# Expert activations made ahead of the transposition, one transposition for two experts, and another order of the down products

## The chip, the cores and the metric

The kernel runs on one core of one Trainium2 chip, in float32. The metric is device microseconds of one execution, the median of several runs. The core's engines work side by side and each takes its own instructions in order: TensorE (PE; its weight loads are shown as PEld), VectorE (DVE), ScalarE (ACT) and the queue of SyncE (SP), which issues the loads.

## The reference

One encoder layer on 512 tokens of width 1024: a mixing sub-layer (a gated short convolution and a latent attention), an attention into a memory of 256 rows, a layer of 16 experts, and a last RMSNorm. The change touches the experts alone. Each expert takes the 64 tokens with the largest affinity to it:

```python
def expert_choice_moe(h, w_router, w_gate, w_up, w_down):
    ...
    gates, idx = lax.top_k(jnp.swapaxes(aff, 1, 2), cap)
    xg = jax.vmap(lambda hb, ib: hb[ib])(h, idx)
    a = jax.nn.silu(jnp.einsum("becd,edf->becf", xg, w_gate)) * jnp.einsum("becd,edf->becf", xg, w_up)
    yo = jnp.einsum("becf,efd->becd", a, w_down) * gates[..., None].astype(h.dtype)
    return jax.vmap(lambda ib, vb: jnp.zeros((s, d), vb.dtype).at[ib.reshape(-1)].add(vb.reshape(-1, d)))(idx, yo)
```

## The kernel before

The sub-layers ahead of the experts and the choice of the tokens take the first 680 us. Then the experts run in eight pairs p, experts 2p and 2p + 1. The weights of a pair come as 24 chunks of 1 MiB ([128, 2048] float32), 16 for gate and up and 8 for down, in the order of their use, through SP's queue. Each chunk has one of 22 equal slots; as soon as a slot is given back after its last product, the next chunk is issued into it (`load_experts`). The order of the instructions on each engine is the order in which the code is written (a manual schedule); waits between engines are semaphores. PSUM banks and the scratch tiles (`scr`, eight buffers) are handed out in turn.

What a pair does, in order:

- `gu_half(e, n)`, for expert e and half n of the 1024 hidden columns: TensorE multiplies the gathered tokens XG (64 of them, as weights) with the gate and the up matrix. The gate product goes to partitions 0 to 63 of one bank and the up product to partitions 64 to 127, side by side in the two halves of the array (L1281, L1282): 8 d tiles, two passes each for float32, in two parts of four d tiles (`gu_part`) between which `mid` stands. Then `gu_evac` copies the bank to SBUF on ScalarE (L1289). The first pair has `gu_wide` in its place, which runs both halves side by side (L1310, L1311).
- `act_half(e, n)`: four transposes of 128x128 on TensorE (L1324, tile guT) bring half n of one expert to [f, (gate, up) of 64 places]; then Silu of the gates on ScalarE (L1329) and the product with the up values on VectorE (L1330) give aT[e], the weights of the down products. They run one step late, as `mid` of the next `gu_half`, and the last of a pair inside the down products.
- `gather(p + 1)`: VectorE makes a one-hot matrix oh (L1241) and the same times the rstd, ohr (L1244); TensorE multiplies the rows of x2 with ohr, one d tile a step (L1249), and VectorE puts each step's bank into XG (L1250). Two steps come behind the last `gu_half` of a pair and two behind each of the first three down steps.
- `down(p)`: four steps of 16 matmuls (L1353), two experts side by side in the array, one half n of d after the other and within it the two halves kh of f; ScalarE and VectorE take each finished half of d out of its bank, times the gates, as a high and a low part (L1359, L1360). `mid`, the last `act_half`, stands ahead of the second step, (n, kh) = (0, 1), which needs it at once.
- In the next pair, behind its first `gu_half`: `pair_prep` (L1259, L1266), then `combine` (L1374), which adds the pair's rows to the tokens' accumulators on VectorE (L1376). The last pair has `tail` in place of gather and combine, which adds and normalises the first half of d under the products of the second.

What a pair of `gu_half` products looks like, and what sets the place of `act_half`:

```python
            PE.matmul(b.t[0:64], lt, wg[:, k], start=kk == 0, stop=kk == KT - 1)
            PE.matmul(b.t[64:128], lt, wu[:, k], start=kk == 0, stop=kk == KT - 1)
...
                gu_half(e, 0, mid=(lambda: act_half(e - 1, 1)) if q else None)
...
                gu_half(e, 1, mid=lambda: act_half(e, 0))
```

Of the kernel before, what the change touches and what calls it, by code (L numbers as in the profile page):

```python
# [18 lines left out]
KT = 8          # 128-row tiles of D  # L19
NT = 4          # 128-row tiles of T  # L20
# [5 lines left out]
SLOT = 2048     # float32 elements per partition and slot  # L26
NSLOT = 22
SPLIT_AHEAD = 2
# slots kept back from the experts' weights; order of the steps that are woven into each other
# [6 lines left out]
# columns of the packed small operands  # L36
# [7 lines left out]
# dense weight entries ([128, 1024] each) in the order of their use  # L44
# [19 lines left out]
def layer_kernel(ctx: ExitStack, tc: tile.TileContext, x, mem, small, rope, dense, experts, out):  # L64
# [42 lines left out]
    def mini(dt, name):  # L107
        """4 KB per partition; three at a time"""
        return minip.tile([128, 1024], dt, name=nm(name), tag="mini")
# [7 lines left out]
    def split(src, hi, lo):  # L117
        """src = hi + lo, both of 12 significant bits"""
        A.copy(hi, src)  # L119
        V.tensor_tensor(lo, src, f32(hi), op=OP.subtract)  # L120

    def split_scaled(src, by, hi, lo):
        """src * by = hi + lo"""
        A.activation(hi, src, AF.Copy, scale=by)
        V.scalar_tensor_tensor(lo, src, by, f32(hi), op0=OP.mult, op1=OP.subtract)

# [12 lines left out]
    def prep_steps(upto, ahead, pieces):  # L139
        """split the entries below upto, a piece at a time; have their chunks, and some more, under way"""  # L140
# [38 lines left out]
    def load_spare():  # L179
        """the last chunk of the first expert goes where there is room beside the slots"""  # L180
        xraw[SPARE] = [scr(name="xs") for _ in range(4)]
        for j, t in enumerate(xraw[SPARE]):
            nc.sync.dma_start(t, experts[SPARE][:, j * 512:(j + 1) * 512])

    class Entry:
        """the split weights of one entry; to be freed after its last use"""
# [11 lines left out]
    class Mac:  # L198
        """products that add up in one piece of a bank"""
# [13 lines left out]
    class Proj:  # L213
        """bank[f, t] = sum over d of W[d, f] * act[d, t], for one 128-column tile of W"""
# [60 lines left out]
    def keep_warm(b, n):  # L275
        """products that nobody reads, against the clock gate of the tensor engine"""
        for _ in range(n):
            PE.matmul(b.t, ones, one.to_broadcast([128, 512]), start=True, stop=True)
# [8 lines left out]
    def rstd_parts(ss, width, n=1):  # L287
        """r, t with r * t = 1 / sqrt(ss / width + eps): the table's root and a Newton step"""
# [25 lines left out]
    def transpose_scaled(rows, g, dst):  # L314
        """rows: list of [128, D] tiles; dst[j] = (hi, lo) of [128, len(rows) * 128]; g per d"""
# [13 lines left out]
    def act_slots(n, name):  # L329
        """[128, 2 (hi, lo), 512] pieces, two to a slot"""  # L330
# [173 lines left out]
    def evac_late(f, b, *args):  # L504
        """evacuate a bank one step later, when its products are done"""
# [10 lines left out]
    def values(n, kt):  # L516
        """values of four heads and 128 keys: [keys, 4 * DV]"""
# [43 lines left out]
    def pair_rope(hp):  # L561
        """rotary queries of two heads; [hi; lo] and [lo; hi] over the partitions"""
# [315 lines left out]
    # values of the memory: [keys, D]  # L878
# [166 lines left out]
    def logits(a, half):  # L1045
        """four products side by side: expert e and k % 4 = g on partition 32 * g + e (the others hold no expert)"""
# [15 lines left out]
    def norm2(a):  # L1062
        """rstd of the rows a: a guess from the bits, a Newton step and one of the third order"""
# [39 lines left out]
    # the C largest affinities of each expert so far, in order, and the next ones behind them: partition e has the  # L1103
    # first 64 of each 128 tokens, partition 32 + e the others
# [24 lines left out]
    def weave(g, other, every=1):  # L1129
        """the steps of g; after some of them one of the other"""  # L1130
# [70 lines left out]
    # the two lists have the C largest at the places i and C - 1 - i, whichever is larger  # L1201
# [35 lines left out]
    def gather(p):  # L1237
        """XG[d, (expert, place)] = x2 * rstd * g of the chosen tokens, one d tile at a time"""
# [15 lines left out]
    def pair_prep(p):  # L1254
        """gates and the transposed one-hot of two experts"""
# [16 lines left out]
    gu_sb, aT = {}, {}  # L1272
# [14 lines left out]
    def gu_evac(e, b, n):  # L1287
        s = scr(name="gu")
        A.copy(s, b.t)  # L1289
        b.free()  # L1290
        gu_sb[e, n] = s
# [9 lines left out]
    def gu_wide(e, then):  # L1301
        """the first two experts: all columns of one d tile after the other, so that a chunk is soon free"""
# [16 lines left out]
    def act_half(e, n):  # L1319
        """silu(gate) * up, transposed to [f, place]"""  # L1320
        s = gu_sb.pop((e, n))
        b = Bank("guT")
        for j in range(4):
            PE.transpose(b.t[:, j * 128:(j + 1) * 128], s[:, j * 128:(j + 1) * 128], ident)  # L1324
        w = b.t.rearrange("p (j s c) -> p j s c", j=4, s=2)
        if n == 0:
            aT[e] = scr(name="aT").rearrange("p (k c) -> p k c", k=KT)
        sg = scr(name="sg")[:, 0:256].rearrange("p (j c) -> p j c", j=4)
        A.activation(sg, w[:, :, 0], AF.Silu)  # L1329
        V.tensor_tensor(aT[e][:, n * 4:n * 4 + 4], w[:, :, 1], sg, op=OP.mult)  # L1330
        b.free()

    def down(p, mid, each, then=None):
        """Y[(expert, place), d] of two experts, times the gates; one half of d after the other"""
        ys = Slot(FR, "y")
        yv = ys.v("n s d", n=2, s=2)
        for n in range(2):
            b = Bank(f"y{n}")
            for kh in range(2):
                cs_ = [xraw.popleft(), xraw.popleft()]  # L1340
                if (n, kh) == (0, 1):
                    mid()
                for kk in range(4):
                    if then is not None:
                        then(n, kh * 4 + kk, yv)
                    k = kh * 4 + kk
                    for q in range(2):
                        if (q, n, kk) == (1, 0, 0) and then is not None:
                            bw = Bank("warm")
                            keep_warm(bw, WARM3)  # L1350
                            bw.free()
                        w = cs_[q].v("k d", k=4)
                        PE.matmul(b.t[q * 64:q * 64 + 64], aT[2 * p + q][:, k], w[:, kk],  # L1353
                                  start=k == 0, stop=k == KT - 1)
                for c in cs_:
                    c.free()
                load_experts(RES_X)
                some(each, GB)
            A.activation(yv[:, n, 0], b.t, AF.Identity, scale=gcol[p])  # L1359
            V.scalar_tensor_tensor(yv[:, n, 1], b.t, gcol[p], f32(yv[:, n, 0]), op0=OP.mult, op1=OP.subtract)  # L1360
            b.free()
# [66 lines left out]
    for p in range(NP):  # L1428
        last = p == NP - 1
        for q in range(2):  # L1430
# [4 lines left out]
            if e == 1:  # L1435
                steps = {1: lambda: act_half(0, 0), 3: lambda: act_half(0, 1), 5: lambda: pair_prep(0)}
                gu_wide(1, lambda k: steps.get(k, int)())
            else:
                gu_half(e, 0, mid=(lambda: act_half(e - 1, 1)) if q else None)
# [12 lines left out]
            if e > 1:  # L1452
                gu_half(e, 1, mid=lambda: act_half(e, 0))
# [5 lines left out]
        if p == 0:  # L1459
            act_half(1, 0)  # L1460

        def mid():
            act_half(2 * p + 1, 1)
# [13 lines left out]
    def last_root(a):  # L1477
        """the parts of the rstd of tile a: the root, and the mean"""
# [33 lines left out]
def _colmajor(w):  # L1512
    """[K, 128 * c] -> per 128-column tile: [c, 128 (row in tile), K / 128 * 128]"""
# [4 lines left out]
def _rowpairs(w):  # L1518
    """[1024, 1024] -> entries (column half, row pair): [8, 128, 2 * 512]"""
# [36 lines left out]
def _experts(i):  # L1556
    gu = np.stack([i["w_exp_gate"][0], i["w_exp_up"][0]], 1)              # e, s, d, f
    gu = gu.reshape(E, 2, 2, 4, 128, 2, 512).transpose(0, 5, 2, 1, 4, 3, 6)  # e, n, kh, s, p, k, f
    dn = i["w_exp_down"][0].reshape(E // 2, 2, 2, 4, 128, 2, 512).transpose(0, 5, 2, 1, 4, 3, 6)  # pair, n, kh, q, p, k, d
    out = np.empty((E // 2, PAIR_CHUNKS, 128, SLOT), np.float32)  # L1560
    out[:, :16] = gu.reshape(E // 2, 16, 128, SLOT)
    wide = np.stack([i["w_exp_gate"][0, :2], i["w_exp_up"][0, :2]], 2)     # e, d, s, f
# [58 lines left out]
```

## Time and profile before

| | |
|---|---|
| runs of the kernel before | 1175.21, 1175.72, 1175.77 us; median 1175.72 |
| span of the profiled execution | 1174.3 us |
| busy share of the span | PE 98%, PEld 66%, DVE 41%, ACT 31% |
| mean granted clock of TensorE | 0.992 of full speed |
| chain that ended last, by line | gate and up products 17% (L1281), down products 11% (L1353), gather 5% (L1249) |
| loads of the experts' weights | 189 of 1 MiB and 8 smaller ones; median 12.6 us from issue to landing for the large ones |

The span runs from the first to the last instruction of one profiled execution; the runs are timed without the profiler, and their median is 1.4 us above that span. All stretches are counted in us from the span's start. A busy TensorE is one with a product in its pipeline. The chain of waits is followed back from the last instruction, at each step to what released it, so its rows on one engine follow each other without a gap where nothing else was waited for. Of the first page's slices, the last 17 (from 675 us) are the experts: there DVE and ACT are busy some one or two tenths, DMA and PE nine in nearly all of them.

### The profile page before, as it was taken

The page shows a single profiled execution, that of the slowest core. Times are in us where ns is not written, and L with a number is a line of the kernel's source. Part 1 is how long each engine was busy: PE and PEld are TensorE (multiplying, and loading weights), DVE is VectorE, ACT ScalarE, POOL GpSimd, SP SyncE. Part 2 cuts the span into 40 slices and gives each one's busy share as a digit, 9 for nine tenths or more (in the row PEclk, how much of TensorE's full clock was granted, in tenths as well). Part 3 has the DMA queues.
Part 4 walks back from the last instruction along what each step waited for, and adds up shares of the span by engine and source line. Part 5 has one row for each costly group of instructions (what it writes and reads, how often), then busy time and mean ns, then how long its engine had stood idle before and what let it go on. Part 6 is the DMA issues. An engine that isn't in the chain of part 4 may idle for free.

```text
span 1174.3 us, 14110 instructions
## 1 busy us (share of the span) xinstructions
PE 1150.4 (98%) x5779; PEld 771.9 (66%) x5779; DVE 484.9 (41%) x942; ACT 364.4 (31%) x672; POOL 1.2 (0%) x5
## 2 busy tenths in 40 slices
PE   8999999999999999999999899999999999999995
PEld 6888888888788888898888544444444444444432
DVE  6567443223588755564555721212121212121204
ACT  6223222223798833564334301100000000000013
POOL 0000000000000000000000000000000000000000
PEclk9999999999999999999999899999999999999998
DMA  8233222222000344234244788899999999999941
GB/s 347 72 108 108 72 75 105 108 108 72 1 36 2 119 168 179 72 133 155 72 180 172 311 317 347 328 417 407 421 421 420 421 421 421 421 421 420 422 188 71
DMA packets 38927, 265.95 MB, mean 226 GB/s; under 512 B 4432, under 2 KB 4816, under 8 KB 8016
## 3 DMA queue, kind: packets, MB, share of 16 engines
q1 hardware_dynamic: 38720, 265.00, 57.0%
q8 instruction: 45, 0.74, 0.3%
q14 instruction: 18, 0.15, 0.0%
q10 hardware_dynamic: 144, 0.07, 0.0%
HBM read 262.95 MB, written 2.10 MB: 226 GB/s over the span
## 4 chain that ended last, share of the span: by engine, by line
PE 93%; DVE 3%; ACT 3%; DMA 0%; issue 0%; SPq 0%; DVEq 0%; ACTq 0%
PE gu L1281 17%; PE y L1353 11%; PE xg L1249 5%; PE mm L205 4%; PE mo L205 4%; PE mq L205 4%; PE mix L205 4%; PE co L205 4%; PE gcv L205 4%; PE gb L205 4%; PE gc L205 4%; PE xc L205 4%; PE gml L205 4%; PE gu L1310 2%; PE cb L1374 2%; PE mk L205 2%
## 5 line engine op out<-in xcount | busy, mean ns | idle before, releaser
L1281 PE MATMUL gu<-xw,xg 128*64 128x512 f32 x448 | 199.8, 596 | 0.0
L1282 PE MATMUL gu<-xw,xg 128*64 128x512 f32 x448 | 199.8, 596 | 0.0
L120 DVE TENSOR_TENSOR ent<-raw,ent 128x1024 fp32r<-128x1024 f32 (+2 forms) x113 | 129.1, 1155 | 92.0 <-ACT ent L119 91.9
L1281 PEld LDWEIGHTS gu<-xw,xg 128*64 128x64 f32 x448 | 58.9, 137 | 117.7 <-issue 115.4
L1353 PE MATMUL y<-xw,aT 128*64 128x512 f32 x512 | 127.4, 599 | 0.0
L119 ACT CAST ent<-raw 128x1024 fp32r<-128x1024 f32 (+2 forms) x113 | 109.1, 996 | 0.0
L1353 PEld LDWEIGHTS y<-xw,aT 128*64 128x64 f32 x512 | 35.8, 136 | 69.1 <-issue 59.8
L1250 DVE TENSOR_SCALAR xg<-xg,small 128x128 f32<-128x128 f32 x64 | 22.5, 351 | 141.1 <-PE xg L1249 141.1
L1249 PEld LDWEIGHTS xg<-ohr,x 128*128 128x128 f32 x512 | 59.8, 191 | 28.8 <-issue 21.1
L1330 DVE TENSOR_TENSOR aT<-guT,sg 128x256 f32<-128x256 f32 x32 | 13.6, 425 | 150.3 <-ACT sg L1329 150.3
L1249 PE MATMUL xg<-ohr,x 128*128 128x128 f32 x512 | 66.4, 282 | 0.4 <-DVE ohr L1244 0.4
L1329 ACT ACTIVATE sg<-guT 128x256 f32<-128x256 f32 x32 | 12.3, 384 | 166.1 <-PE guT L1324 166.1
L1289 ACT COPY gu<-gu 128x512 f32<-128x512 f32 x32 | 18.8, 586 | 145.0 <-PE gu L1282 110.9
L1282 PEld LDWEIGHTS gu<-xw,xg 128*64 128x64 f32 x448 | 58.9, 137 | 0.0
L205 PE MATMUL mm<-ent,mo 128*128 128x512 f32 x192 | 48.4, 399 | 0.0
L205 PE MATMUL gcv<-hT,ent 128*128 128x512 f32 x192 | 44.8, 389 | 0.0
L205 PE MATMUL co<-yT,ent 128*128 128x512 f32 x192 | 44.8, 389 | 0.0
L205 PE MATMUL gb<-hT,ent 128*128 128x512 f32 x192 | 44.8, 389 | 0.0
L205 PE MATMUL gc<-hT,ent 128*128 128x512 f32 x192 | 44.8, 389 | 0.0
L205 PE MATMUL xc<-hT,ent 128*128 128x512 f32 x192 | 44.8, 389 | 0.0
L205 PE MATMUL mq<-hm,ent 128*128 128x512 f32 x192 | 44.7, 390 | 0.0
L205 PE MATMUL mo<-o,ent 128*128 128x512 f32 x192 | 44.7, 391 | 0.0
(276 smaller groups left out, 1717.4 us busy)
## 6 DMA issues: line engine op xcount, KB each, us to landing
xw<-in_experts_dram SPq DMA_DIRECT2D x189, 1024.0 KB, 12.6
raw<-in_dense_dram SPq DMA_DIRECT2D x52, 1024.0 KB, 4.8
x<-in_x_dram SPq DMA_DIRECT2D x8, 512.0 KB, 4.5
xw<-in_experts_dram SPq DMA_DIRECT2D x4, 512.0 KB, 16.1
out_dram<-out SPq DMA_DIRECT2D x4, 512.0 KB, 2.6
raw<-in_dense_dram SPq DMA_DIRECT2D x2, 512.0 KB, 8.1
mem<-in_mem_dram SPq DMA_DIRECT2D x1, 1024.0 KB, 5.0
xs<-in_experts_dram SPq DMA_DIRECT2D x4, 256.0 KB, 15.0
```

The costliest lines, as they stand in the source:

```text
L119: A.copy(hi, src)
L120: V.tensor_tensor(lo, src, f32(hi), op=OP.subtract)
L205: PE.matmul(self.o, lhsT, rhs, start=self.k == 0, stop=self.k == self.n - 1)
L1249: PE.matmul(b.t[:, 0:128], xt[a][:, k * 128:(k + 1) * 128], w[:, a], start=a == 0, stop=a == NT - 1)
L1250: V.tensor_scalar(XG[p][:, k], b.t[:, 0:128], col(S_GMOE + k), None, op0=OP.mult)
L1281: PE.matmul(b.t[0:64], lt, wg[:, k], start=kk == 0, stop=kk == KT - 1)
L1282: PE.matmul(b.t[64:128], lt, wu[:, k], start=kk == 0, stop=kk == KT - 1)
L1289: A.copy(s, b.t)
L1310: PE.matmul(bs[n].t[0:64], lt, w[n], start=k == 0, stop=k == KT - 1)
L1330: V.tensor_tensor(aT[e][:, n * 4:n * 4 + 4], w[:, :, 1], sg, op=OP.mult)
L1353: PE.matmul(b.t[q * 64:q * 64 + 64], aT[2 * p + q][:, k], w[:, kk], start=k == 0, stop=k == KT - 1)
L1374: PE.matmul(b.t, OHT[p][:, a * 128:(a + 1) * 128], yv[:, n, s], start=s == 0, stop=s == 1)
```

## The change

- `gu_evac` no longer copies the bank. It takes Silu of the gate half on ScalarE (64x512, from partitions 0 to 63 to a scratch tile's partitions 64 to 127) and multiplies it with the up half on VectorE, into act[p, n]: the first expert of the pair to partitions 0 to 63, the second to 64 to 127.
- `act_trans(p, n)` takes the place of `act_half(e, n)`: four transposes of act[p, n], which hold both experts, and copies out of the bank to aT[p, n]: for n = 0 one on ScalarE, for n = 1 two of 256 columns on VectorE. So a pair has two groups of transposes instead of four: n = 0 as `mid` of the second half of the second expert, n = 1 ahead of the second down step. In the first pair n = 0 stands behind the gather's two steps.
- `down`: for all pairs but the last, kh is the outer loop and n the inner one, with two banks open; so the first two steps read aT[p, 0] and the last two aT[p, 1]. Both halves of d are taken out at the end of their second step. The chunks lie in HBM in that order. The last pair keeps the order of before.
- Comments were left out of the whole file, which moves nothing.

```diff
-    gu_sb, aT = {}, {}
+
...
     def gu_evac(e, b, n):
-        s = scr(name="gu")
-        A.copy(s, b.t)
-        b.free()
-        gu_sb[e, n] = s
+
+        p, q = divmod(e, 2)
+        if q == 0:
+            act[p, n] = scr(name="act")
+        sg = scr(name="sg")
+        A.activation(sg[64:128], b.t[0:64], AF.Silu)
+        V.tensor_tensor(act[p, n][q * 64:q * 64 + 64], b.t[64:128], sg[64:128], op=OP.mult)
+        b.free()
 
...
-    def act_half(e, n):
-        """silu(gate) * up, transposed to [f, place]"""
-        s = gu_sb.pop((e, n))
-        b = Bank("guT")
+    def act_trans(p, n):
+
+        s = act.pop((p, n))
+        b = Bank("actT")
         for j in range(4):
             PE.transpose(b.t[:, j * 128:(j + 1) * 128], s[:, j * 128:(j + 1) * 128], ident)
-        w = b.t.rearrange("p (j s c) -> p j s c", j=4, s=2)
+        aT[p, n] = scr(name="aT").rearrange("p (j c) -> p j c", j=4)
+        w = b.t.rearrange("p (j c) -> p j c", j=4)
         if n == 0:
-            aT[e] = scr(name="aT").rearrange("p (k c) -> p k c", k=KT)
-        sg = scr(name="sg")[:, 0:256].rearrange("p (j c) -> p j c", j=4)
-        A.activation(sg, w[:, :, 0], AF.Silu)
-        V.tensor_tensor(aT[e][:, n * 4:n * 4 + 4], w[:, :, 1], sg, op=OP.mult)
+            A.copy(aT[p, n], w)
+        else:
+            for h in range(2):
+                V.tensor_copy(aT[p, n][:, 2 * h:2 * h + 2], w[:, 2 * h:2 * h + 2])
         b.free()
 
     def down(p, mid, each, then=None):
-        """Y[(expert, place), d] of two experts, times the gates; one half of d after the other"""
+
+
         ys = Slot(FR, "y")
         yv = ys.v("n s d", n=2, s=2)
-        for n in range(2):
-            b = Bank(f"y{n}")
-            for kh in range(2):
-                cs_ = [xraw.popleft(), xraw.popleft()]
-                if (n, kh) == (0, 1):
-                    mid()
-                for kk in range(4):
-                    if then is not None:
-                        then(n, kh * 4 + kk, yv)
-                    k = kh * 4 + kk
-                    for q in range(2):
-                        if (q, n, kk) == (1, 0, 0) and then is not None:
-                            bw = Bank("warm")
-                            keep_warm(bw, WARM3)
-                            bw.free()
-                        w = cs_[q].v("k d", k=4)
-                        PE.matmul(b.t[q * 64:q * 64 + 64], aT[2 * p + q][:, k], w[:, kk],
-                                  start=k == 0, stop=k == KT - 1)
-                for c in cs_:
-                    c.free()
-                load_experts(RES_X)
-                some(each, GB)
-            A.activation(yv[:, n, 0], b.t, AF.Identity, scale=gcol[p])
-            V.scalar_tensor_tensor(yv[:, n, 1], b.t, gcol[p], f32(yv[:, n, 0]), op0=OP.mult, op1=OP.subtract)
-            b.free()
+        bs = {}
+        order = [(n, kh) for n in range(2) for kh in range(2)] if then else [(n, kh) for kh in range(2) for n in range(2)]
+        for i, (n, kh) in enumerate(order):
+            if n not in bs:
+                bs[n] = Bank(f"y{n}")
+            b = bs[n]
+            cs_ = [xraw.popleft(), xraw.popleft()]
+            if i == 1:
+                mid()
+            for kk in range(4):
+                if then is not None:
+                    then(n, kh * 4 + kk, yv)
+                k = kh * 4 + kk
+                for q in range(2):
+                    if (q, n, kk) == (1, 0, 0) and then is not None:
+                        bw = Bank("warm")
+                        keep_warm(bw, WARM3)
+                        bw.free()
+                    w = cs_[q].v("k d", k=4)
+                    PE.matmul(b.t[q * 64:q * 64 + 64], aT[p, kh][:, kk, q * C:(q + 1) * C], w[:, kk],
+                              start=k == 0, stop=k == KT - 1)
+            for c in cs_:
+                c.free()
+            load_experts(RES_X)
+            some(each, GB)
+            if kh == 1:
+                A.activation(yv[:, n, 0], b.t, AF.Identity, scale=gcol[p])
+                V.scalar_tensor_tensor(yv[:, n, 1], b.t, gcol[p], f32(yv[:, n, 0]), op0=OP.mult, op1=OP.subtract)
+                b.free()
         return ys, yv
 
...
             if e == 1:
-                steps = {1: lambda: act_half(0, 0), 3: lambda: act_half(0, 1), 5: lambda: pair_prep(0)}
-                gu_wide(1, lambda k: steps.get(k, int)())
+                gu_wide(1, lambda k: pair_prep(0) if k == 5 else None)
             else:
-                gu_half(e, 0, mid=(lambda: act_half(e - 1, 1)) if q else None)
...
             if e > 1:
-                gu_half(e, 1, mid=lambda: act_half(e, 0))
+                gu_half(e, 1, mid=(lambda: act_trans(p, 0)) if q else None)
...
         if p == 0:
-            act_half(1, 0)
+            act_trans(0, 0)
 
         def mid():
-            act_half(2 * p + 1, 1)
+            act_trans(p, 1)
             if last:
...
-    out[:, 16:] = dn.reshape(E // 2, 8, 128, SLOT)
+    out[:-1, 16:] = dn[:-1].transpose(0, 2, 1, 3, 4, 5, 6).reshape(E // 2 - 1, 8, 128, SLOT)
+    out[-1, 16:] = dn[-1].reshape(8, 128, SLOT)
```

On VectorE, in the second pair, about the end of the second expert's gate and up products and the start of the next gather. The numbers tell tiles of one name apart; what waits is in brackets. Before:

```order
L1330 TENSOR_TENSOR aT_5827<-guT_5858,sg_5863 128x256 [waits Activation_49]
L1330 TENSOR_TENSOR aT_5898<-guT_5893,sg_5899 128x256 [waits DVE_49,Activation_49]
L1241 TENSOR_TENSOR oh_5916<-plT_5419,small_75 128x512
L1244 TENSOR_TENSOR ohr_5917<-oh_5916,r_721_4967 128x512 [waits DVE_49]
L1250 TENSOR_SCALAR xg_5920<-xg_5921,small_75 128x128 [waits PE_49]
```

After:

```order
L1294 TENSOR_TENSOR act_5747<-gu_5827,sg_5852 64x512 [waits Activation_49]
L1294 TENSOR_TENSOR act_5823<-gu_5855,sg_5887 64x512 [waits Activation_49]
L1241 TENSOR_TENSOR oh_5890<-plT_5419,small_75 128x512
L1244 TENSOR_TENSOR ohr_5891<-oh_5890,r_721_4967 128x512 [waits DVE_49]
L1250 TENSOR_SCALAR xg_5894<-xg_5895,small_75 128x128 [waits PE_49]
```

Ahead of oh stood the product of the second expert's first half, which follows a transposition in the middle of the last gate and up products; now the product of its second half (act from the bank gu_5855) stands there, which follows the last of them. What follows, the evacuation of the gather's steps, stands as before.

On TensorE, in the same pair, from the end of the gather's second pair of steps to the first matmuls of the second down step. Before:

```order
L1249 MATMUL xg_5951<-ohr_5917,x_3169 128x128
L1249 MATMUL xg_5951<-ohr_5917,x_3170 128x128 x2
L1324 MATMUL guT_5957<-small_75,gu_5914 128x128 [waits Activation_49]
L1324 MATMUL guT_5957<-small_75,gu_5914 128x128 x3
L1353 MATMUL y_926_5934<-xw_5746,aT_5827 64x512 [waits DMAHW1_49]
L1353 MATMUL y_926_5934<-xw_5756,aT_5898 64x512 [waits DMAHW2_49,DVE_49]
```

After:

```order
L1249 MATMUL xg_5925<-ohr_5891,x_3169 128x128 x2
L1249 MATMUL xg_5925<-ohr_5891,x_3170 128x128 x2
L1328 MATMUL actT_5932<-small_75,act_5823 128x128 [waits Activation_49]
L1328 MATMUL actT_5932<-small_75,act_5823 128x128 x3
L1362 MATMUL y_922_5931<-xw_5733,aT_5873 64x512 [waits DMAHW1_49,PE_49]
L1362 MATMUL y_922_5931<-xw_5743,aT_5873 64x512 [waits DMAHW2_49]
```

The four transposes stand at the same place, but the matmuls behind them go to the other bank (y_922) and read aT_5873, which was transposed a good step earlier, where before the second expert's (aT_5898) read what had just been transposed; its wait for VectorE is gone. On the same engine the two groups of transposes of the first expert, in the middle of its second half and in the middle of the second expert's first half, have no counterpart.

## Rows read from the trace of the kernel before

**Rows 1.** Stretches: us, PE, PEld, DVE, ACT, POOL busy (instructions), PEclk, DMA share, GB/s.
```profile
1080.00:1120.00 40.00, 40.00 (x214) 20.21 (x212) 9.55 (x20) 4.49 (x8) 0.00 (x0) 1.00 1.01 421
1120.00:1160.00 40.00, 39.17 (x158) 12.98 (x158) 6.78 (x14) 7.38 (x16) 0.00 (x0) 1.00 0.23 91
```

**Rows 2.** Chain of waits, 898 to 988 us: start us, us, engine, tile, line.
```profile
898.42 1.98 PE xg L1249 x16
...
906.41 4.64 PE y L1353 x16
...
918.59 3.58 PE y L1353 x16
...
929.04 0.98 PE gcol L1259 x8
...
945.38 0.59 PE guT L1324 x4
...
952.99 0.59 PE guT L1324 x4
...
987.78 0.98 PE gcol L1259 x8
```

**Rows 3.** Waits, 650 us to the end: who waited for whom, us, times, longest.
```profile
PEld y L1353 <- DVE aT L1330: 6.9, 8, 0.9
```

**Rows 4.** Groups, 700 to 1160 us: operation, shapes, count | busy us, mean ns | idle before.
```profile
L1376 DVE TENSOR_TENSOR acc<-cb,acc 128x512 f32<-128x512 f32 x48 | 29.3, 682 | 3.8 <-PE cb L1374 3.8
L1289 ACT COPY gu<-gu 128x512 f32<-128x512 f32 x32 | 18.8, 586 | 145.0 <-PE gu L1282 110.9 <-PE gu L1311 34.1
L1330 DVE TENSOR_TENSOR aT<-guT,sg 128x256 f32<-128x256 f32 x32 | 13.6, 425 | 150.3 <-ACT sg L1329 150.3
L1329 ACT ACTIVATE sg<-guT 128x256 f32<-128x256 f32 x32 | 12.3, 384 | 166.1 <-PE guT L1324 166.1
L1360 DVE SCALAR_TENSOR_TENSOR y<-y,gcol,y 128x512 fp32r<-128x512 f32 x15 | 11.2, 747 | 34.3 <-ACT y L1359 34.3
L1359 ACT ACTIVATE y<-y,gcol 128x512 fp32r<-128x512 f32 x15 | 10.3, 687 | 107.3 <-PE y L1353 107.3
```

**Rows 5.** VectorE in order of time, 895 to 897 us: start, us, instruction [idle before].
```profile
895.29 0.42 DVE L1330 TENSOR_TENSOR aT<-guT,sg 128x256 f32<-128x256 f32 x1 [7.18 <-ACT sg L1329]
895.63 0.68 DVE L1241 TENSOR_TENSOR oh<-plT,small 128x512 f32<-128x512 f32 x1
896.35 0.69 DVE L1244 TENSOR_TENSOR ohr<-oh,r 128x512 f32<-128x512 f32 x1
```

**Rows 6.** ScalarE in order of time, 894 to 899 us.
```profile
894.87 0.38 ACT L1329 ACTIVATE sg<-guT 128x256 f32<-128x256 f32 x1 [3.40 <-PE guT L1324]
898.47 0.59 ACT L1289 COPY gu<-gu 128x512 f32<-128x512 f32 x1 [3.21 <-PE gu L1282]
```

**Rows 7.** Chain of waits at the first gather, where TensorE waits for ohr.
```profile
679.79 0.70 DVE ohr L1244
680.50 0.14 issue
680.63 2.02 PE xg L1249 x16
```

**Rows 8.** Stretches round two falls of the granted clock; columns as in rows 1.
```profile
5.00:12.00 7.00, 4.28 (x23) 2.45 (x22) 4.85 (x18) 5.51 (x14) 0.00 (x0) 1.00 0.98 367
12.10:15.40 3.30, 3.14 (x15) 2.73 (x14) 3.26 (x7) 2.12 (x5) 0.00 (x0) 0.50 0.99 415
660.00:667.30 7.30, 5.21 (x39) 3.28 (x37) 5.55 (x37) 2.97 (x10) 0.00 (x0) 1.00 0.99 369
667.40:674.10 6.70, 4.53 (x7) 1.97 (x8) 5.53 (x29) 2.34 (x6) 0.00 (x0) 0.50 1.00 421
674.20:681.00 6.80, 5.00 (x22) 2.61 (x21) 4.29 (x17) 0.00 (x0) 0.00 (x0) 1.00 1.00 410
```

**Rows 9.** TensorE in order of time, ahead of each fall [idle before].
```profile
10.18 1.09 PE L348 MATMUL tr<-small,hs 128*128 128x128 f32 x8 [1.74 <-DVE tiny L291]
...
669.57 0.37 PE L1115 MATMUL affT<-small,aff 128*16 128x128 f32 x1 [3.37 <-DVE aff L1100]
```

More of the change, by code (lines that the diff above doesn't have):

```diff
@@ L1269, in pair_prep @@
         b.free()
-    gu_sb, aT = {}, {}
+    act, aT = {}, {}
     def gu_part(e, b, kh):
@@ L1435, in layer_kernel @@
             if e == 1:
-                steps = {1: lambda: act_half(0, 0), 3: lambda: act_half(0, 1), 5: lambda: pair_prep(0)}
-                gu_wide(1, lambda k: steps.get(k, int)())
+                gu_wide(1, lambda k: pair_prep(0) if k == 5 else None)
             else:
-                gu_half(e, 0, mid=(lambda: act_half(e - 1, 1)) if q else None)
+                gu_half(e, 0)
             if q == 0:
```

## The prediction

> **What bounds the kernel now.** I read the stretches of the expert stage first, since the whole diff lies there (from about 680 us to the end). TensorE is busy for all of 40.00 us in every stretch up to 1120, at the full granted clock [rows 1], and the chain of waits runs through its products without a break [rows 2]. The same rows show the loads close behind: 421 GB/s. A pair of experts is 24 chunks of 1 MiB, 25.17 MB, so 59.8 us at that rate, while a pair takes 987.78 − 929.04 = 58.74 us [rows 2]. So the loads have been losing 1.1 us a pair against a lead. That lead is still large at the end: the rate falls to a mean of 91 GB/s from 1120 to 1160 [rows 1], 3.6 MB or some 9 us of loading, while the last down products run until about 1160. TensorE sets the end, not the loads, and a pair that takes 59 us or more hardly touches the lead.
>
> **The change part by part.** The sum is made per pair on the profiled execution (span 1174.3 us; the median of the runs, 1175.72, is 1.4 above it, and I carry this over).
>
> *Transpositions that go.* A pair had four groups of four transposes, now it has two. Two that stood inside gate/up products go; the one in the second half of the second expert and the one in the down products stay. What such a group costs is read from the gap between two of them: 952.99 − 945.38 = 7.61 us with one half of gate/up products and one group in it, against 929.04 − (918.59 + 3.58) = 6.87 us for a half without one [rows 2]. So 0.74 us each: 0.59 for the transposes and 0.15 for the break in the paired products. Two of them: −1.48 us in each of eight pairs, all on TensorE's path.
>
> *The wait in the down products.* The second step of them takes 4.64 us where another takes 3.58 [rows 2], since it waits for the half of aT that has only just been transposed: 6.9 us over 8 waits [rows 3]. With the new order the second step takes the other columns with the first half of aT, and the new half is wanted a step and two gather steps (5.6 us) later; two copies of 256 columns, below the 425 ns of the product of that size [rows 4], lie well within that. −0.9 in pairs 0 to 6. Pair 0 has a second such wait, ahead of its first step, of which about 0.2 goes (one copy of 586 ns instead of 384 + 425 [rows 4]). In the last pair the old order stands, filled with other products, and nothing is won there.
>
> *Products that move ahead of the transposition.* Per half: one Silu and one product of 64x512, instead of a copy of 128x512 and then a Silu and a product of 128x256. Three of the four halves have a further 3.4 us (half of 6.87) of products ahead of whatever needs them, so they cost nothing; if that cover were gone, each would cost the 1.37 us of its Silu and product worked out below. A PSUM bank is held longer by that product, 0.7 us, with others to take in turn meanwhile.
>
> *The wait that is added.* The fourth half (second expert, second half) ends the gate/up products, and the next thing on TensorE is the gather of the next pair, whose product reads ohr. VectorE makes oh and ohr, in the order in which it was told. Before, its last instruction ahead of them was the product of a transposition in the middle of that half, so oh ran at 895.63 and ohr at 896.35, done by 897.04, and TensorE went on at 898.42 without a gap [rows 2, 5]. Now the product of this last half stands ahead of oh, and it waits for Silu, which waits for the last gate/up product. Queued behind the waiting product: oh, ohr, the gather's evacuations; and for ohr waits TensorE, which has nothing else in order. From the end of the last product: ScalarE starts 0.05 later (898.42 to 898.47) [rows 2, 6]; Silu over 512 columns is not in the trace, its neighbours are the copy of that shape, 586 ns, and the activation with a scale, 687, so I take 0.60; the product starts 0.04 after it (894.87 + 0.38 to 895.29) [rows 5, 6]; over 512 columns from PSUM it is like acc, 682 ns, and oh starts 0.08 before its end as after aT: 0.60; oh to ohr 0.72, ohr 0.69 [rows 5]; ohr's end to the first gather product 0.14 [rows 7]. Sum: 0.05 + 0.60 + 0.04 + 0.60 + 0.72 + 0.69 + 0.14 = 2.84 us of idle TensorE. Bounds: with Silu and product at the cost of half the columns (0.38 and 0.43 − 0.08) 2.37; with the scaled activation and y's 0.75 without overlap 3.08. I keep 2.84, nearest to rows of the same width. Seven pairs have it, 0 to 6; the last gathers nothing.
>
> *Sum so far.* Pairs 1 to 6: −1.48 − 0.9 + 2.84 = +0.46, six times: +2.8. Pair 0: 0.2 less: +0.3. Pair 7: −1.48. Together +1.6 us: 1177.3. So the work shed and the wait added almost cancel. With the bounds of the wait: −1.7 to +3.3, 1174.0 to 1179.0.
>
> *The clock.* An idle stretch of 2.84 us in otherwise dense products isn't in the trace, but two falls of the granted clock are. In 5 to 12 us TensorE was busy 4.28 of 7.00 us at clock 1.00 (one idle of 1.74 us among it), and from 12.1 to 15.4 the clock is 0.50, that is 1.2 GHz instead of 2.4. In 660 to 667.3 it was busy 5.21 of 7.30 us and from 667.4 to 674.1 it is 0.50 again, the fall coming about 1.2 us into an idle of 3.37 us. From 674.2 to 681 it was busy 5.00 of 6.80 and kept 1.00 [rows 8, 9]. So 2.7 and 2.1 us of idle, in pieces, stood ahead of the falls, and 1.8 us brought none. The idle here is longer than any of these and in one piece, and I expect a fall after most of the seven. It came at different distances from the idle, so not after each: I take five. Price of a fall: with TensorE busy again at once, as from 12.1 to 15.4 (3.14 of 3.30 us), the low stretch is 3.3 us, half of which is lost: 1.65 us. The other lasted 6.7, but TensorE was idle for its first 2.2 us. Bounds: nothing, and 3.35 each. Five times 1.65 is 8.2 us. A pair with a fall takes some 60.9 us, so the loads stay ahead.
>
> Sum: 1175.7 + 1.6 + 8.2 = **1185.5 us**.
>
> The Trainium skill speaks against the last term (TensorE: Matmul & The Clock Gate, "Why this matters for your kernels"): it asks that idles between bursts of matmuls stay below a limit, and 2.84 us lies just below it, so by that rule no fall comes and the sum stays at 1177.3. The rows above show falls after shorter idles that stood close together, so I keep the term, and the rule has its chance as the first rival.
>
> **The rivals.** *The clock holds.* The seven waits are there, but no fall or at most one or two follow. For it: no idle as long as this with dense products on both sides is in the trace, and the stretch up to 681 kept its clock with 1.8 us of idle. Against it: the two falls. Time: 1177.3, up to 1180 with a fall or two.
>
> *Longer low stretches.* Each idle ends in a fall, and the clock stays low for 6.7 us as from 667.4: 7 x 3.35 = 23 us, 1200. Against it: TensorE is dense after each wait.
>
> *The wait is short (the other side: faster).* Place: between the last gate/up product of a pair and the first gather product. If oh and ohr were not held behind the product there (or the chain were half as long, 1.4 us), no fall would follow and each of the seven pairs would gain some 1.0 us net: 1175.7 + 1.6 − 7 x 1.44 = 1167. It turns faster than before when the idle is below 2.6 us with no fall. Against it: the order of VectorE's instructions puts both behind the product, ohr has to follow oh, and only widths could make the chain shorter, to 2.37.
>
> *The change doesn't do what it says* only in the last pair, where the order of the down products is as before; this is in the sum.
>
> **How the numbers follow.** Waits with three to seven falls of 1.65: 0.62 (1182 to 1189). The clock holds: 0.27 (1174 to 1180). Longer low stretches: 0.06. Short wait: 0.05. The likeliest gives 1185.5. The range for 8 in 10 takes in the forecast and the upper part of the first rival and leaves out the short wait, the long stretches and the lowest end of the bounds: 1176.5 to 1190. Against 1175.72, 0.2% is 2.35 us, about what a measurement of this kernel can tell from no change. Slower: the forecast, the long stretches and the part of the first rival above 1178.07: 0.62 + 0.06 + 0.08 = 0.76. Same: most of the rest of that rival: 0.18. Faster: 0.06.
>
> **What would show it.** Right: 16 groups of transposes instead of 32, none between the halves of a first expert; second down step at 3.58 us; TensorE idle 2.7 to 3.0 us ahead of the gather, released by VectorE's ohr, seven times; the granted clock below 1.00 after most of them, with the expert stage's pairs at 59.2 us without a fall and 60.9 with one. Wrong: no such idle (the order argument fails), the idle but a clock of 1.00 throughout (the first rival), or TensorE waiting for chunks, which would say that the lead of the loads was misjudged.

## The result, and the profile after

| | before | after |
|---|---|---|
| median of the runs compared | 1175.74 us | 1183.59 us (1183.13 to 1183.92) |
| span of the profiled execution | 1174.3 us | 1182.1 us |
| mean granted clock of TensorE | 0.992 | 0.989 |
| transposition groups in the expert stage | 32 | 16 |

The change makes the kernel slower: ratio 1.0067, 95% interval 1.0052 to 1.0081, or 7.9 us. The forecast was 1185.5 with a range of 1176.5 to 1190.

The waits of TensorE name the place first (line waited for, and what it waited for: us in total, times, longest us):

```profile
PE xg L1249 <- DVE ohr L1244: 20.5, 8, 2.9
```

One of the eight is the 0.4 us of the first gather, which the kernel before has too; the other seven stand at the end of each pair but the last. The chain of waits shows one of them (start us, us, engine, tile, line), where [rows 2] had products without a break:

```profile
874.51 0.98 PE gcol L1259 x8
...
901.15 0.02 issue
901.17 0.60 ACT sg L1293
901.77 0.02 issue
901.79 0.69 DVE act L1294
902.49 0.03 issue
902.52 0.70 DVE oh L1241
903.22 0.02 issue
903.25 0.70 DVE ohr L1244
903.95 0.04 issue
903.99 2.05 PE xg L1249 x16
...
912.05 3.58 PE y L1362 x16
...
933.63 0.98 PE gcol L1259 x8
...
994.38 0.98 PE gcol L1259 x8
```

Read the second part downwards: the last gate/up product ends, and then four instructions on two other engines run one after the other before TensorE has anything to do. The chain leaves TensorE only where it waits, so such a ladder of other engines' rows in an expert stage that had none is the added wait itself. The second down step, at 912.05, now takes 3.58 us instead of the 4.64 of [rows 2].

The stretches of three of these idles, and of what follows each, tell the rest (from:to, length; busy time and instructions of PE, PEld, DVE, ACT, POOL; granted clock; DMA share; GB/s):

```profile
719.30:722.30 3.00, 0.13 (x3) 0.06 (x1) 2.66 (x4) 0.59 (x1) 0.00 (x0) 1.00 1.01 429
722.30:729.30 7.00, 6.33 (x38) 3.56 (x39) 0.70 (x2) 0.58 (x1) 0.00 (x0) 1.00 0.46 192
779.60:782.60 3.00, 0.13 (x3) 0.05 (x1) 2.08 (x3) 0.59 (x1) 0.00 (x0) 1.00 1.03 429
782.80:786.20 3.40, 3.40 (x18) 3.18 (x19) 0.40 (x2) 0.00 (x0) 0.00 (x0) 0.50 1.01 422
1081.70:1084.70 3.00, 0.13 (x3) 0.07 (x1) 2.08 (x3) 0.59 (x1) 0.00 (x0) 1.00 1.02 426
1084.70:1092.00 7.30, 7.30 (x48) 4.65 (x49) 1.05 (x3) 0.00 (x0) 0.00 (x0) 1.00 1.01 421
```

TensorE is idle for 2.87 us in each; behind the second one the granted clock is 0.50 (1.2 GHz) for 3.4 us, behind the first and the last it stays at 1.00 (2.4 GHz). Such a drop of the granted clock is called a fall below. In this execution the clock fell after four of the seven (at 782.8, 844.3, 963.7 and 1025.2 us). From one gcol to the next in the chain, a pair without a fall takes 59.11 or 59.12 us (874.51 to 933.63) and one with a fall 60.71 to 60.77 (933.63 to 994.38), against 58.73 before: a fall costs 1.63 us.

The groups of the new instructions, 870 to 990 us (as [rows 4]):

```profile
L1294 DVE TENSOR_TENSOR act<-gu,sg 64x512 f32<-64x512 f32 x8 | 5.5, 694 | 50.1 <-ACT sg L1293 50.1
L1293 ACT ACTIVATE sg<-gu 64x512 f32<-64x512 f32 x8 | 4.7, 588 | 51.2 <-PE gu L1282 51.2
L1335 DVE COPY aT<-actT 128x256 f32<-128x256 f32 x4 | 1.5, 420 | 0.2
```

Silu and product have half the partitions of the copy and of acc in [rows 4] and take as long (588 against 586, 694 against 682 ns), while Silu and product over half the columns took 384 and 425 ns [rows 4]: here the columns set the time, not the partitions.

Where the 7.8 us between the spans lie, by the starts of gcol: the part up to the first gcol is 1.44 us shorter (two groups of pair 0); pair 0's stretch 1.63 longer (the idle, less what its first two down steps no longer wait); pairs 1 to 6 are 0.38 us longer each, 2.3 in all, and the four falls come on top with 6.5; the part behind the last gcol is 1.2 shorter. −1.44 + 1.63 + 2.3 + 6.5 − 1.2 = 7.8.

### The profile page after: what moved, and what is told of

Its sections match the earlier page's. It is cut to its first block, busy times and chain, and to the rows that moved or that the text cites. A ratio compares the mean times of both kernels' runs of the same rounds, so it can differ in the third digit from the quotient of the medians.

```text
span 1182.1 us, 13968 instructions
## 1 busy us (share of the span) xinstructions
PE 1135.1 (96%) x5715; PEld 767.9 (65%) x5715; DVE 500.0 (42%) x958; ACT 356.6 (30%) x648; POOL 1.2 (0%) x5
## 4 chain that ended last, share of the span: by engine, by line
PE 92%; DVE 4%; ACT 3%; DMA 0%; issue 0%; SPq 0%; DVEq 0%
PE gu L1281 16%; PE y L1362 10%; PE xg L1249 6%; PE mm L205 4%; PE mq L205 4%; PE mo L205 4%; PE mix L205 4%; PE co L205 4%; PE gb L205 4%; PE gc L205 4%; PE gcv L205 4%; PE xc L205 4%; PE gml L205 4%; PE gu L1314 2%; PE cb L1384 2%; PE mk L205 2%
## 5 line engine op out<-in xcount | busy, mean ns | idle before, releaser
L1282 PE MATMUL gu<-xw,xg 128*64 128x512 f32 x448 | 196.8, 594 | 0.0
L1281 PE MATMUL gu<-xw,xg 128*64 128x512 f32 x448 | 196.8, 594 | 0.0
L1362 PE MATMUL y<-xw,aT 128*64 128x512 f32 x512 | 121.3, 608 | 0.7 <-ACT aT L1332 0.7
L1294 DVE TENSOR_TENSOR act<-gu,sg 64x512 f32<-64x512 f32 x32 | 22.2, 694 | 186.5 <-ACT sg L1293 186.4
L1249 PEld LDWEIGHTS xg<-ohr,x 128*128 128x128 f32 x512 | 63.5, 201 | 49.4 <-DVE ohr L1244 26.2
L1249 PE MATMUL xg<-ohr,x 128*128 128x128 f32 x512 | 70.6, 293 | 20.5 <-DVE ohr L1244 20.5
L1293 ACT ACTIVATE sg<-gu 64x512 f32<-64x512 f32 x32 | 18.8, 588 | 213.3 <-PE gu L1282 179.3
L1369 ACT ACTIVATE y<-y,gcol 128x512 fp32r<-128x512 f32 x16 | 11.0, 687 | 183.7 <-PE y L1362 183.7
```

Source lines behind the costliest of these rows:

```text
L1249: PE.matmul(b.t[:, 0:128], xt[a][:, k * 128:(k + 1) * 128], w[:, a], start=a == 0, stop=a == NT - 1)
L1293: A.activation(sg[64:128], b.t[0:64], AF.Silu)
L1294: V.tensor_tensor(act[p, n][q * 64:q * 64 + 64], b.t[64:128], sg[64:128], op=OP.mult)
L1362: PE.matmul(b.t[q * 64:q * 64 + 64], aT[p, kh][:, kk, q * C:(q + 1) * C], w[:, kk], start=k == 0, stop=k == KT - 1)
```

## The experiments

**Theory.** Fewer transposes and the new order of the down products save about as much as the idles ahead of the gather cost; the loss that is left is the clock's, and it follows from the idles. **Rivals.** The idles have another cause than VectorE's order; the falls have nothing to do with the idles or cost nothing; the loads bind. All medians below are of runs beside those of the kernel before on the same chip (its median 1175.5 to 1176.3 us).

**The one-hots made early.** The kernel after, with the two instructions on VectorE put ahead of the last evacuation's product:

```diff
         V.tensor_tensor(w, w0, r2[:, :, None].to_broadcast([128, NT, 128]), op=OP.mult)
+        yield
...
-                gu_half(e, 1, mid=(lambda: act_trans(p, 0)) if q else None)
+                if q and not last:
+                    gat = gather(p + 1)
+
+                def half():
+                    act_trans(p, 0)
+                    if not last:
+                        next(gat)
+
+                gu_half(e, 1, mid=half if q else None)
...
```

The first pair, which has no such half, makes them at step 6 of `gu_wide`.

> The kernel after, with oh and ohr of the next pair made on VectorE in the middle of the last gate/up half of a pair (beside the transposition there), instead of behind the product of that half's evacuation. Theory (the 2.87 us idles come from that order, and the falls of the clock from the idles): no idle ahead of the gather, granted clock 1.00 through the expert stage, so 1183.6 - 7 x 2.87 - 4 x 1.63 = 1157.0 us, pairs of 56.2 us. Rival (the loads bind, since 24 chunks take 59.7 us and a pair now takes less): TensorE waits for chunks near the end, 1159 to 1168 us. Rival (the idles have another cause): 1180 or more, idles still there.

Measured: 1157.09 us, ratio 0.9836 (0.9823 to 0.9850). VectorE in order of time at the end of a pair, and TensorE's clock from 700 to 1100 us (columns as above):

```profile
882.82 0.69 DVE L1241 TENSOR_TENSOR oh<-plT,small 128x512 f32<-128x512 f32 x1
883.55 0.69 DVE L1244 TENSOR_TENSOR ohr<-oh,r 128x512 f32<-128x512 f32 x1
889.67 0.70 DVE L1295 TENSOR_TENSOR act<-gu,sg 64x512 f32<-64x512 f32 x1 [5.43 <-ACT sg L1294]
```
```profile
700.00:900.00 200.00, 199.32 (x1043) 90.77 (x1041) 49.95 (x99) 18.25 (x30) 0.00 (x0) 1.00 0.98 400
900.00:1100.00 200.00, 200.00 (x1042) 92.49 (x1039) 51.67 (x101) 17.86 (x29) 0.00 (x0) 1.00 1.01 421
```

oh and ohr are done 5.4 us ahead of the product that they stood behind, in time in which VectorE waited anyway; TensorE is busy for all but 0.7 of 400 us and its clock is 1.00. A pair takes 56.19 us. So the order of two instructions on VectorE was worth 26.5 us: seven idles and four falls. The loads don't bind, but their lead shrinks: the second down chunk of the last pair lands 6.0 us ahead of its first product, where it was 20.2 before, and no chunk of that pair has less.

**The same edit in the kernel before.**

> The kernel before with oh and ohr made in the middle of the last gate/up half, the same edit as in e1_early_onehot. In the kernel before TensorE did not wait for them. Theory (the edit only takes away the wait that the change had added): 1176.2 us, no difference. Rival (making them early is a gain of its own): 1170 us or less.

Measured: 1175.46 us, ratio 1.0000 (0.9991 to 1.0009). Early one-hots are no gain of their own; they only undo a wait.

**The wait alone, in the kernel before.**

```diff
         A.copy(s, b.t)
+        if e % 2 and n and e < E - 1:
+            V.tensor_tensor(scr(name="late")[64:128], b.t[64:128], s[0:64], op=OP.mult)
         b.free()
```

> The kernel before with the wait alone: behind the copy of the last gate/up half of pairs 0 to 6 VectorE multiplies the two halves of that bank's rows (64x512, nobody reads the result), so oh and ohr come as late as in the kernel after; transpositions and order of the down products as before. Theory: seven idles of 2.8 to 2.9 us, 20 us, and a fall of the clock after three to five of them at 1.63 us: 1175.7 + 20 + 4.9 to 8.2 = 1200.6 to 1203.9 us. Rival (idles cost only themselves): 1195.7 us, clock 1.00. Rival (the idle of the kernel after comes from elsewhere): no idle, 1176 us.

Measured: 1206.19 us (1202.15 to 1209.38), ratio 1.0247 (1.0226 to 1.0269). Its waits, and two of the stretches at low clock:

```profile
PE xg L1249 <- DVE ohr L1244: 20.7, 8, 3.0
```
```profile
789.30:792.60 3.30, 3.30 (x13) 1.82 (x13) 0.58 (x2) 0.00 (x0) 0.00 (x0) 0.50 1.03 425
850.70:854.00 3.30, 2.77 (x13) 2.77 (x14) 0.82 (x2) 0.00 (x0) 0.00 (x0) 0.50 0.99 412
```

The idles are those of the kernel after, so the cause of them is shown from both sides. But the profiled execution (1206.6 us) has a fall at each of the seven, where I expected three to five, and the median lies 2.3 us above the upper end of the range that I expected. Why all seven fall here is open, and it need not be so in each execution: the five differ by 7.2 us, with a granted clock of 0.990 in the shortest and 0.981 in the longest. The second row holds 0.5 us without a product: there the clock fell before TensorE went on, and such a fall costs a little less than 1.63 (pairs of 63.0 us against 63.2).

**The idle filled.** The kernel after, with three unread products in each idle:

```diff
+        if not last:
+            bw = Bank("warm")
+            keep_warm(bw, 3)
+            bw.free()
         some(gat, GA)
```

> The kernel after, with three products of 128x512 in float32 that nobody reads put on TensorE in each of the seven idles ahead of the gather (at some 0.86 us each 2.6 of 2.87 us). Theory (the falls come from the idles): no fall in the expert stage, pairs of 59.1 us, 1183.6 - 4 x 1.63 = 1177.1 us. Rival (the falls have another cause, or cost nothing): 1183.6 us, clock 0.50 after some gathers as before.

Measured: 1177.16 us, ratio 1.0009 (1.0000 to 1.0018). TensorE at the end of a pair, and its clock:

```profile
957.70 2.85 PE L278 MATMUL warm<-one 128*128 128x512 f32 x6
960.64 0.60 PE L1249 MATMUL xg<-ohr,x 128*128 128x128 f32 x3
```
```profile
700.00:900.00 200.00, 198.98 (x1002) 89.11 (x1003) 46.42 (x91) 18.23 (x30) 0.00 (x0) 1.00 0.97 391
900.00:1100.00 200.00, 199.65 (x1024) 92.29 (x1024) 48.58 (x97) 15.39 (x25) 0.00 (x0) 1.00 1.01 421
```

The gather starts as late as before, no work was saved, and yet the kernel is 6.4 us faster than after: four falls of 1.63 are 6.5. This separates the two costs of the idle. The change without its falls is the kernel before to 0.1%.

**The order of the down products alone, in the kernel before** (the loop over n and kh as in the change, with the chunks in that order).

> The kernel before with the other order of the down products alone (pairs 0 to 6, with the chunks in that order). Theory: the second down step no longer waits for aT, 3.58 us instead of 4.64, -0.9 us a pair: 1175.7 - 7 x 0.9 = 1169.4 us. Rival (the wait moves to a later step, or the loads bind): 1174 to 1176 us.

Measured: 1169.26 us, ratio 0.9938 (0.9926 to 0.9951): −1.0 us a pair. The chain of one pair:

```profile
925.15 0.98 PE gcol L1259 x8
...
961.22 3.58 PE y L1356 x16
...
982.80 0.98 PE gcol L1259 x8
```

The second down step takes 3.58 us, and the pair 57.65 instead of 58.74 [rows 2].

**The old order of the down products, with early one-hots.**

> The kernel with oh and ohr made early (e1_early_onehot), and the down products of all pairs in their old order (with the chunks in that order). The new half of aT is then wanted right behind its transposition, as in the kernel before, but now it comes by copies of 256 columns (0.42 us) instead of a Silu and a product. Theory: a wait of about 0.5 us in the second down step (0.03 + 0.42 + some 0.08), seven times: 1157.1 + 3.5 = 1160.6 us. Rival (the wait is that of the kernel before, 0.9 to 1.0): 1163.4 to 1164.1 us. Rival (the order is worth nothing here, since the loads bind): 1157 us.

Measured: 1160.52 us, ratio 0.9869 (0.9854 to 0.9884), +3.4 us. The chain at the second down step:

```profile
898.44 0.45 PE actT L1329 x4
898.89 0.02 issue
898.92 0.43 DVE aT L1336
899.35 0.04 issue
899.39 3.65 PE y L1363 x16
```

With activations multiplied ahead of the transposition only a copy stands between transposes and products: the wait is 0.5 us instead of 1.06. So the order is worth 1.0 us a pair by itself (1.1 by the gcol rows) and 0.5 to 0.6 with the rest of the change (0.5 by the medians, 0.6 by the gcol rows, 56.78 against 56.19): the two edits share a part of their gain.

**The transposition groups given back, with early one-hots** (two unread groups of four in each pair, at the old places).

> The kernel with oh and ohr made early (e1_early_onehot), and in each of the eight pairs two groups of four transposes of 128x128 that nobody reads, at the places where the change took two away (the middle of the first expert's second half and of the second expert's first half). Theory (a group costs 0.74 us, 0.59 for itself and 0.15 for the break in the paired products): 1157.1 + 16 x 0.74 = 1168.9 us. Rival (a break costs nothing, a group 0.59): 1166.5 us. Rival (the time goes by the loads, a group costs nothing): 1157 to 1159 us.

Measured: 1168.73 us, ratio 0.9938 (0.9926 to 0.9951): +11.6 us, 0.73 each. The chain of a pair:

```profile
925.66 0.98 PE gcol L1260 x8
...
934.36 0.59 PE extra L1327 x4
941.97 0.59 PE extra L1327 x4
...
983.31 0.98 PE gcol L1260 x8
```

57.65 us a pair against 56.19 without them: 0.73 each, of which 0.59 are the transposes. The rest is the break in the paired products: the first of them behind a group takes 0.57 us in the chain, where the others take 0.42.

**A shorter and a longer idle.** The kernel after with oh early and ohr not (one `yield` between the two lines), and the kernel after with one more unread one-hot on VectorE ahead of oh.

> The kernel after, with oh alone made early in the middle of the last gate/up half; ohr stays behind the product of the evacuation. Seven idles of 2.87 - 0.72 = 2.15 us remain. Theory: 1183.6 - 7 x 0.72 = 1178.6 us if the clock falls four times as before, 1172.1 us if it does not fall; I expect two falls, 1175.3 us. Rival (falls are a matter of the products, not of the length of the idle): four falls, 1178.6 us.

> The kernel after, with one more one-hot of 128x512 (0.72 us, nobody reads it) on VectorE ahead of oh in the seven gathers behind pair 0's. Idles of 2.87 + 0.72 = 3.59 us. Theory (a longer idle brings a fall more often): 1183.6 + 7 x 0.72 = 1188.6 us with four falls, 1193.5 us with seven; I expect six, 1191.9 us. Rival (four falls whatever the length): 1188.6 us.

Measured: 1176.46 us (1174.97 to 1178.98), ratio 1.0005 (0.9997 to 1.0014); and 1195.12 us (1192.82 to 1195.58), ratio 1.0158 (1.0144 to 1.0172). The shorter one's waits, a low stretch and the stretch behind it, then the longer one's waits and its two longest low stretches:

```profile
PE xg L1250 <- DVE ohr L1245: 15.4, 8, 2.1
```
```profile
783.80:787.10 3.30, 3.30 (x13) 1.84 (x14) 0.58 (x2) 0.00 (x0) 0.00 (x0) 0.50 1.00 417
787.20:1019.10 231.90, 223.34 (x1160) 101.72 (x1157) 56.73 (x111) 19.60 (x32) 0.00 (x0) 1.00 1.01 417
```
```profile
PE xg L1253 <- DVE ohr L1248: 24.7, 8, 3.5
```
```profile
722.60:732.70 10.10, 8.63 (x30) 5.47 (x32) 1.40 (x4) 0.58 (x1) 0.00 (x0) 0.50 0.36 152
787.40:794.10 6.70, 5.66 (x22) 4.21 (x24) 1.65 (x4) 0.00 (x0) 0.00 (x0) 0.50 1.01 418
```

Idles of 2.1 us still bring the clock down, three times in the profiled execution (1177.0 us; at 722, 784 and 1019), with a stretch of 232 us at 1.00 between that holds four equal idles; only behind the last of them the clock falls again. Idles of 3.5 us bring six falls, and two of them last 6.7 and 10.1 us. I expected two and six. The longer kernel lies 3.2 us above the 1191.9 expected with six falls; by the gcol starts its two long low stretches cost some 3.6 us more than falls of 1.63 would. Among the three variants of the kernel after, a longer idle went with more falls (three, four and six of seven, in one profiled execution each), but 2.89 us in the kernel before brought seven, so the length alone doesn't set the number, and the times scatter with it (4 us among runs of the shorter one). In the four kernels with falls in the expert stage (the kernel after, the kernel before with the wait, the shorter and the longer idle) each of these falls began between 1.1 us ahead of the end of an idle and 1.5 us behind it; the two long stretches are those that began earliest, 1.1 and 0.9 us ahead. What tells two equal idles of one kernel apart stays open.

**One transposition moved to the gather.** With early one-hots, and the group for aT[p, 0] between the first two gather steps instead of in the middle of the gate/up products:

```diff
+                def half():
+                    if last:
+                        act_trans(p, 0)
+                    else:
+                        next(gat)
...
-        some(gat, GA)
-        if p == 0:
-            act_trans(0, 0)
...
+        some(gat, 1)
+        if not last:
+            act_trans(p, 0)
+        some(gat, GA - 1)
```

> The kernel with oh and ohr made early (e1_early_onehot), and in pairs 0 to 6 the transposition of the first half of aT moved out of the gate/up products to a place between the first two gather steps, where no paired products are broken. Theory (a group costs 0.74 us within the paired products and 0.44 us next to a gather step, as the one in the down products does): -0.3 us a pair, 7 times: 1157.1 - 2.1 = 1155.0 us. Rival (the copy of aT comes too late for the first down step, or the loads bind, whose lead was down to 6 us): 1157 to 1159 us.

Measured: 1153.26 us, ratio 0.9813 (0.9799 to 0.9826), the fastest of all. The chain of a pair:

```profile
942.21 1.09 PE xg L1250 x8
943.30 0.44 PE actT L1329 x4
943.74 0.89 PE xg L1250 x8
944.63 3.58 PE y L1363 x16
...
972.22 0.98 PE gcol L1260 x8
```

The group takes 0.44 us here, and the next gather step hides its copy. From the gcol at 916.31 the pair takes 55.91 us, −0.28; with 0.74 in pair 0, where a wait for aT goes too, this is −2.4 us. The rest of the difference between the medians (3.8) doesn't lie in the edit: the part ahead of the experts was 0.7 us shorter in this execution, and the kernel before 0.8 us faster beside these runs. The chunk that landed 6.0 us ahead of its product with early one-hots alone lands 4.3 us ahead here.

## Why the prediction was right, and where its sizes were off

- **What bounds the kernel.** TensorE bounds it, as predicted: it waits for no chunk in the expert stage after, and with early one-hots TensorE is busy throughout, although a pair then takes less than the loads need. The lead pays for it, as argued.
- **Transposes.** The prediction took 0.74 us a group from the gap between two rows; 0.73 was measured with the groups given back, and the last pair's stretch from gcol to its first down step is 1.48 us shorter, the two groups. The part behind the last gcol gained only 1.2, because 4.0 us follow VectorE's last instruction instead of 3.7.
- **The wait in the down products.** The gain of 0.9 was too small: the waits' row [rows 3] gives what PEld waited for, but the step itself was 1.06 longer (4.64 against 3.58, [rows 2]), and the order alone gained 1.0 a pair. The pair of steps on the path was the better row. This is why a pair without a fall came out at +0.38 and not at +0.46; a part of the 0.16 was taken back, since the gather steps behind the idle take 2.05 us instead of 1.98 and the idle is 0.03 longer. Without falls the spans differ by 7.8 − 6.5 = 1.3 us, for 1.6 in the sum, so these errors cancel in part.
- **Products ahead of the transposition.** They cost nothing in three halves of four: TensorE waits nowhere for them. The 0.7 us that it waits in pair 0's first down step are for the copy of aT, and the prediction had kept that wait, 0.2 us shorter than before. With early one-hots, which take the fourth half off the path, the pair is 58.73 − 2 x 0.74 − 1.06 = 56.19 us, to the hundredth what that kernel shows.
- **The added wait.** The prediction had 2.84 us, and 2.87 was measured. Its ladder is the sum term by term: Silu takes 0.60 for 0.60; from the product's start to oh's it is 0.73 for 0.60, since oh doesn't start ahead of the product's end; from oh to ohr 0.73 for 0.72; from ohr's start to the gather 0.74 for 0.69 + 0.14 of [rows 5, 7]. The parts were off by up to 0.13, in different directions, so a part of the agreement is luck.
- **The clock.** The price was right (1.65 from the low stretch of [rows 8], 1.63 measured), and the count was five for four. These 8.2 for 6.5 are nearly all of the 1.9 us between forecast and result; all other terms together were 0.3 too high. That falls would come followed from the rows, but the count was a guess, and that it lay only one off is luck: for the kernel before with the wait I expected three to five and seven came. The trace before holds a third fall, which the prediction doesn't count, at 1165.7 us behind the last down products; the kernel after has one there too (at 1175.4), so it adds nothing to the difference.
- **The rivals.** The clock did not hold. The Trainium skill (TensorE: Matmul & The Clock Gate, "Why this matters for your kernels") asks that idles between bursts of matmuls stay below a limit that 2.87 us lies just below; the falls after four of seven, and after three of seven idles of 2.1 us, speak against taking it as a safe bound here, and the measurement decides. The longer low stretches did not come either: all four lasted 3.4 us, and in the expert stage only two falls at idles of 3.5 us lasted 6.7 and 10.1. The short wait would have needed the other order on VectorE: with it the kernel does become faster, 1157.09.

The order argument, the idle's length, the falls' price and the price of a group are shown by runs that change one of them alone. Not shown is why the clock falls after some idles and not after others, and so how many falls a kernel will have.

## What to carry to other kernels

When an evacuation grows from a copy into a chain of two engines, look at what is queued behind its last instruction on the slower engine: here two instructions that needed none of it held up TensorE, and putting them earlier turned a change of +0.7% into one of −1.6%. An idle of TensorE has two prices, itself and the clock afterwards; products that nobody reads, put into it, tell the two apart in one run. A group of transposes is cheapest where it breaks no paired products.

## What the runs showed of the hardware

- Equal idles within one execution can end differently: in one profiled execution each, 2.87 us brought a fall in four of seven, 2.1 us in three of seven, 3.5 us in six of seven, and 2.9 to 3.0 us in the kernel before with the wait in seven of seven. A fall among dense products lasted 3.4 us as a rule, but 10.1 and 6.7 at two of the 3.5 us idles.
- Four transposes of 128x128 took 0.59 us between paired gate/up products, with 0.14 more for the break, and 0.44 us between gather steps.
- Silu and product of 64x512 (588 and 694 ns) took as long as a copy and a sum of 128x512 (586 and 682 ns).
